# A planned two-layer decoder trunk on one core: score matmuls, weight splits and convolution chains are issued in another order

## The chip, the cores and the metric

The kernel runs on one core of one Trainium2 chip. The metric is the device time of one execution in microseconds (us); the kernel before takes 1359.83 us, the median of three runs (1359.78 to 1360.3).

## The reference, cut to what matters

Two layers work on 256 tokens of width 1024, all in float32. Each layer is, in this order, a SwiGLU feed-forward block (FFN1, inner width 2752), a mixer, a second SwiGLU block (FFN2) and a gated per-layer embedding (PLE); each block starts with an RMS norm and adds to the residual stream:

```python
z = u @ w_in                      # mLSTM q|k, v, o-gate, gates; SWA q, k, v; merge gates
m_qk = silu(causal_dwconv(m_qk, m_conv_w, m_conv_b))          # 4 taps
hm = mlstm_chunkwise(mq, mk, mv, ig, lf)                      # 4 heads of 256
ha = swa_gqa_sinks(aq, ak, av, a_sinks)                       # 16 query heads, 4 kv heads of 64
merged = sigmoid(g_m) * (hm @ w_branch_m) + sigmoid(g_a) * (ha @ w_branch_a)
h = h + merged @ w_out
```

## The kernel before, in words

Every float32 matrix product is made of three products of rounded halves: a value x is split into hi (a rounded copy) and lo = x - hi, and a product is hi·hi + hi·lo + lo·hi. The split of a weight part (128 rows by 1024 columns) takes one copy `wh` on ScalarE and one subtraction `wl` on VectorE; both read the tile `raw` that a DMA on the SyncE queue has filled. There are two raw tiles (`RAW`) and eight pairs of split tiles (`RING`). The same split is made of every activation that is multiplied, as `uT` (the normed, transposed residual), `qT` (queries of the window attention), `qk` (convolved queries and keys of the mLSTM) and `hmT` (output of the mLSTM heads).

The order of instructions on TensorE, ScalarE, VectorE and SyncE is that of the Python program, which carries a planner. `Clock` holds an estimated time for each engine; `now` is that of TensorE. Small work stands in generators ("chains") in the list `bg`: a chain issues one step, yields, and is due again when its step should be done. Between matmuls the program calls `tick()`, which advances every chain that is due and then calls `feed()`, which may begin the split of one more weight part: it issues `wh` and leaves a chain that will issue `wl`. `feed()` holds back while ScalarE's or VectorE's estimated end is more than 3.0 us past `now` (2.0 us once four parts are in store: `AHEAD`, `STORE`). `finish(chain)` is called where TensorE is about to need a chain's result; it moves the planner's clock to the next due time until the chain is done. When a raw tile's last `wl` has been issued, `prefetch()` issues the next load.

The chains that the change touches:

- `conv` (line 1158), 8 in each layer: four ScalarE activations in a first step for the two chains of a projection (`cv`, bias and last tap), then two steps of three VectorE multiply-adds each, a Silu on ScalarE (`cy`), and the split of the result (`qk`). `qk_job` starts two of them at the end of each of the four `z` projections. The key half ends in the chain `head`, which does an mLSTM head: `st` matmuls, weighting, `num` matmuls, a norm, transposes into `hmT`. Heads pass in order (`begun`, `turn`). The output gate `og` has to be there before `num`.
- `scores` (line 1361): for a block of 128 queries and a pair of kv heads. Two steps of 12 matmuls (two query heads, both kv heads) for the second block, one of 24 for the first. The queries' hi and lo halves are in `qT`; the two kv heads of a pair lie on different halves of the partitions.
- `norm` (line 639): after the last block of a layer and before the next FFN1 (`between`), it scales, then transposes (`to_T`) and splits into `uT`.

After the mixer's first two `z` projections comes `ya` (attention output times w_branch_a), then `og`, two more `z`, the gate `gt`, and `ym` (hm times w_branch_m, whose last k tiles are head 3's `hmT`).

Of the kernel before, what the change touches and what calls it, by code (L numbers as in the profile page):

```python
# [19 lines left out]
P = 128  # L20
# [14 lines left out]
RING = 8  # L35
STORE, HASTE = 4, 3
AHEAD = (3.0, 2.0)
ACTIVE = 5
LAG = 1.5
WARM = 5  # L40
# [126 lines left out]
class Trunk:  # L167
# [7 lines left out]
    def __init__(self, ctx, tc, a, out):  # L175
        self.tc, self.a, self.out = tc, a, out
        self.clock = Clock()
        self.nc = Core(self.clock, tc.nc)
        pool = lambda name, bufs, **k: ctx.enter_context(tc.tile_pool(name=name, bufs=bufs, **k))
        self.const = pool("const", 1)  # L180
        self.rawp = pool("raw", RAW)
        self.wp = pool("w", RING)
        self.slots = pool("slots", 22)
        self.gp = pool("g", 1)
        self.sc = pool("sc", 7)
        self.small = pool("small", 6)
        self.psum = pool("psum", 8, space=PSUM)
        self.dram = pool("dram", 1, space=bass.MemoryType.DRAM)
        self.n = 0
        self.jobs, self.bg, self.haste, self.second = [], [], False, None  # L190
        self.embedded, self.crossed, self.extra = {}, False, 0
        self.pending, self.loaded, self.store = deque(), deque(), 0
        self.free, self.raws = deque([0.0] * RING), deque([0.0] * RAW)
        self.consts()
# [5 lines left out]

    def tick(self):

        for chain in list(self.bg):
            if chain[1] <= self.clock.now:
                self.advance(chain)
        self.feed()

    def advance(self, chain):
        if chain not in self.bg:
# [3 lines left out]
            self.bg.remove(chain)  # L213
        chain[1] = self.clock.end(outer)

    def later(self, chain, ready=0.0):

        self.bg.append([chain, max(self.clock.done(), ready)])
        return self.bg[-1]

    def start(self, chain):
        chain = self.later(chain)
        self.advance(chain)
        return chain

    def finish(self, chain):
        while chain in self.bg:
            self.tick()
            ahead = [c[1] for c in self.bg if c[1] > self.clock.now]
            if ahead and chain in self.bg:  # L230
                self.clock.wait(min(ahead))

# [103 lines left out]
    def feed(self, must=False):  # L336

        clock = self.clock
        if not self.loaded or not self.free:
            return  # L340
        raw, parts = self.loaded[0]
        part, arrival = parts[0]
        slack = AHEAD[self.store >= STORE]
        if not must and max(self.free[0], arrival, clock.t["scalar"] - slack, clock.t["vector"] - slack) > clock.now:
            return
        if not must and (self.second is not None or self.haste and self.store >= HASTE + self.extra):
            return
        self.store += 1
        ready = max(self.free.popleft(), arrival)
        parts.popleft()  # L350
        last = not parts
        if last:
            self.loaded.popleft()
        w = part.k * part.n
        hi = self.wp.tile([P, QU], F32R, tag="wh", name=self.name("wh"))[:, :w]
        lo = self.wp.tile([P, QU], F32R, tag="wl", name=self.name("wl"))[:, :w]

        def chain():
            src = raw[:, part.c0 : part.c0 + w]
            if part.gain is not None:  # L360
                for j in range(part.k):
                    o = slice(j * part.n, (j + 1) * part.n)
                    self.nc.scalar.mul(hi[:, o], src[:, o], part.gain[:, j : j + 1])
                yield
                for j in range(part.k):
                    o = slice(j * part.n, (j + 1) * part.n)
                    self.nc.vector.scalar_tensor_tensor(lo[:, o], src[:, o], part.gain[:, j : j + 1],
                                                        hi[:, o].bitcast(F32), op0=ALU.mult, op1=ALU.subtract)
            elif part.rows is None:
                yield from self.splitting(hi, lo, src)  # L370
            else:
                self.tc.nc.gpsimd.memset(lo[part.rows.stop :].bitcast(F32), 0.0)
                self.nc.scalar.copy(hi, src)
                yield
                r = part.rows
                self.nc.vector.tensor_tensor(lo[r], src[r], hi[r].bitcast(F32), op=ALU.subtract)
            part.ready = clock.done()
            if last:
                self.raws.append(part.ready)
                self.prefetch()  # L380

        part.hi, part.lo = (x.rearrange("p (k n) -> p k n", k=part.k) for x in (hi, lo))
        part.chain = self.later(chain())
        outer = clock.begin(dma=ready)
        self.advance(part.chain)
        clock.end(outer)
        return part.chain

    def need(self, part):

# [248 lines left out]
    def norm(self, t, ss, g, xT, between):  # L639

        r = self.scale(ss)
        if between and t:
            self.clock.stage["late"] = self.clock.done() + LAG
        yield
        xn = [self.scaled(t, n, r, g) for n in range(2)]
        if between and t:
            self.clock.stage["late"] = self.clock.done() + LAG
        yield
        while between and not self.crossed:
            yield  # L650
        for n in range(2):
            self.to_T(xn[n], xT, n * 4, t)
        if t == 0:
            self.haste = False
# [395 lines left out]
class Mlstm:  # L1050
# [97 lines left out]
    def qk_job(self, w_in, part, hp):  # L1148

        c0 = part * D + hp * NB  # L1150
        unit = self.tr.unit(w_in, c0)

        def run():
            for i, ps in enumerate(self.tr.project_T(unit, self.xT, "z")):
                self.tr.start(self.conv(ps, part, 2 * hp + i, c0 // P + 2 * i))
        self.tr.jobs.append(run)

    def conv(self, ps, part, hd, f):
# [106 lines left out]
class Swa:  # L1265
# [83 lines left out]
    def groups(self, chains):  # L1349
        tr, acc = self.tr, {}  # L1350
        for p in range(2):
            for t in range(NT):
                while any(self.inputs.get(i, tr) is tr or self.inputs[i] in tr.bg
                          for i in [(0, s) for s in range(t + 1)] + [(p + 1, t)]):
                    yield
                while sum(c in tr.bg for c in chains) >= ACTIVE:
                    yield
# [3 lines left out]
    def scores(self, t, p, acc, chains):  # L1361


        tr, nc = self.tr, self.nc
        S = (t + 1) * P
        per = NB // S
        tok = slice(t * P, (t + 1) * P)
        rows = [slice(g * AD, (g + 1) * AD) for g in range(2)]
# [4 lines left out]
        for j0 in range(0, 4, per):  # L1373
            js = slice(j0, j0 + per)
            ps = [tr.bank("sc").rearrange("p (j s) -> p j s", j=per) for _ in range(2)]
            for j in range(per):
                for x, y in ((0, 0), (0, 1), (1, 0)):
                    for g in range(2):
                        nc.tensor.matmul(ps[g][:, j, :], self.qT[x](4 * p + j0 + j, tok, p=rows[g]),
                                         self.kT[rows[g], y, p, :S], start=j + x + y == 0, stop=x == 1,  # L1380
                                         skip_group_check=True)
            yield
            if t:
                for g in range(2):
                    nc.scalar.copy(pr[g][:, js, :], ps[g][:, :, P:])
                yield
            for g in range(2):
                if t:
                    above = tr.above.bitcast(mybir.dt.uint32)[:, None, :].to_broadcast([P, per, P])
                    nc.vector.copy_predicated(pr[g][:, js, :], above, ps[g][:, :, :P])  # L1390
                    nc.vector.tensor_reduce(mx[g][:, js], pr[g][:, js, :], axis=AX.X, op=ALU.max)
                else:
                    for j in range(per):
                        i = j0 + j
                        nc.vector.tensor_tensor_reduce(pr[g][:, i, :], ps[g][:, j, :], tr.band, 1.0, NEG, op0=ALU.add,
                                                       op1=ALU.max, accum_out=mx[g][:, i : i + 1])
                nc.vector.scalar_tensor_tensor(mx[g][:, js], mx[g][:, js], -0.125, self.nsink[:, hd[g]][:, js],
                                               op0=ALU.mult, op1=ALU.min)
            yield
            for g in range(2):  # L1400
                for j in range(per):
                    i = j0 + j
                    nc.scalar.activation(pr[g][:, i, :], pr[g][:, i, :], AF.Exp, scale=0.125, bias=mx[g][:, i : i + 1],
                                         accum_out=den[g][:, i : i + 1])
# [79 lines left out]
```

## Time and profile before

| what | value |
|---|---|
| median of three runs | 1359.83 us |
| the profiled execution's own time | 1359.88 us |
| its span, first to last instruction | 1358.2 us |
| TensorE matmul busy | 1350.5 us, 99% |
| VectorE busy | 903.0 us, 66% |
| ScalarE busy | 751.0 us, 55% |
| granted TensorE clock | 1.000 |
| chain that ended last | TensorE 97%, VectorE 2% |

The profiled execution lies 0.05 us above the median, and 1.7 us of its time lie outside the span. Matmul ends are modelled, and matmuls overlap; so the time that a wait costs is best read from starts: how much longer a group of matmuls takes from its start to the start of the next than the same group elsewhere. In the rows, "PE" is TensorE's matmuls, "PEld" its weight loads, "DVE" VectorE, "ACT" ScalarE; nearly all instructions carry line 133, the planner's helper, so the tile names tell them apart.

### The profile page before, as it was taken

Reading aid. Unit: us, or ns where it says so; the run is one execution under the profiler, and the core shown is the slowest. Engines: PE = TensorE matmul, PEld = TensorE weight load, DVE = VectorE, ACT = ScalarE, POOL = GpSimd, SP = SyncE. Lnnn points to the kernel's source line nnn. Section 1 sums busy time; section 2 is a strip of 40 time slices with the busy share of each in tenths; the row PEclk is TensorE's granted clock in tenths of the full one; section 3 lists DMA queues with packets and bytes.
Section 4 is the critical chain, followed back from the end, with each engine's and each line's share of the span. In section 5 each row is a group of like instructions: output and inputs, shape, how many; then the busy total and the mean of one; then the engine's idle time right before and its main releaser. Section 6 shows DMA issues by size and latency. Waiting matters only on the chain.

```text
span 1358.2 us, 22024 instructions
## 1 busy us (share of the span) xinstructions
PE 1350.5 (99%) x8974; PEld 1223.5 (90%) x8974; DVE 903.0 (66%) x1411; ACT 751.0 (55%) x1241; POOL 53.4 (4%) x82
## 2 busy tenths in 40 slices
PE   9999999999999999999999999999999999999998
PEld 7999887899899899988889998878998998999887
DVE  6766567888887755454665554578888877554545
ACT  6655446887565444443555443468875654444433
POOL 1000003000000000000000000030000000000000
PEclk9999999999999999999999999999999999999999
DMA  7755745354654475565466556463546554755651
GB/s 239 226 187 158 248 146 195 117 156 124 219 202 163 153 234 185 172 223 182 169 217 216 173 193 200 136 203 107 160 120 221 199 174 143 244 188 171 235 192 54
DMA packets 126789, 245.91 MB, mean 181 GB/s; under 512 B 15160, under 2 KB 24288, under 8 KB 126688
## 3 DMA queue, kind: packets, MB, share of 16 engines
q1 hardware_dynamic: 126672, 244.50, 55.9%
q8 instruction: 70, 1.15, 0.3%
q14 instruction: 31, 0.25, 0.1%
q10 hardware_dynamic: 16, 0.00, 0.0%
HBM read 242.39 MB, written 2.10 MB: 180 GB/s over the span
## 4 chain that ended last, share of the span: by engine, by line
PE 97%; DVE 2%; ACT 0%; DMA 0%; issue 0%; SPq 0%; DVEq 0%; ACTq 0%
PE dn L133 18%; PE pg L133 18%; PE pu L133 14%; PE gu L133 7%; PE gt L133 7%; PE z L133 7%; PE kvq L133 5%; PE og L133 3%; PE yo L133 3%; PE ym L133 3%; PE v L133 3%; PE tp L133 3%; PE ya L133 2%; PE sc L133 1%; DVE cv L133 1%; PE ha L133 1%
## 5 line engine op out<-in xcount | busy, mean ns | idle before, releaser
L133 DVE TENSOR_TENSOR wl<-raw,wh 128x1024 fp32r<-128x1024 f32 (+1 forms) x405 | 487.9, 1221 | 272.3 <-ACT wh L133 270.0
L133 ACT CAST wh<-raw 128x1024 fp32r<-128x1024 f32 x405 | 415.2, 1049 | 329.5 <-DMA raw<-in_ffn_w_down_dram 71.2
L133 PE MATMUL dn<-wh,hid 128*128 128x512 f32 x688 | 218.1, 395 | 0.0
L133 PE MATMUL pg<-uT,wh 128*128 128x256 f32 x1088 | 195.0, 282 | 0.0
L133 PE MATMUL pu<-uT,wh 128*128 128x256 f32 x1088 | 193.9, 281 | 0.0
L133 PEld LDWEIGHTS pg<-uT,wh 128*128 128x128 f32 x1088 | 166.8, 188 | 0.4
L133 PEld LDWEIGHTS pu<-uT,wh 128*128 128x128 f32 x1088 | 166.4, 188 | 0.0
L133 PEld LDWEIGHTS dn<-wh,hid 128*128 128x128 f32 x688 | 129.2, 188 | 30.7
L133 PE MATMUL pg<-uT,wl 128*128 128x256 f32 x544 | 152.6, 280 | 0.0
L133 PE MATMUL pu<-uT,wl 128*128 128x256 f32 x544 | 152.5, 280 | 0.0
L133 PE MATMUL dn<-wl,hid 128*128 128x512 f32 x352 | 139.2, 395 | 0.0
L133 PEld LDWEIGHTS pu<-uT,wl 128*128 128x128 f32 x544 | 102.7, 189 | 0.0
L133 PEld LDWEIGHTS pg<-uT,wl 128*128 128x128 f32 x544 | 102.7, 189 | 0.0
L133 PE MATMUL gt<-uT,wh 128*128 128x256 f32 x512 | 92.8, 282 | 0.0
L133 PE MATMUL z<-uT,wh 128*128 128x256 f32 x512 | 92.6, 283 | 0.0
L133 PE MATMUL gu<-wh,uT 128*128 128x512 f32 x256 | 81.4, 399 | 0.0
L133 PEld LDWEIGHTS gt<-uT,wh 128*128 128x128 f32 x512 | 79.1, 188 | 1.5
L133 PEld LDWEIGHTS dn<-wl,hid 128*128 128x128 f32 x352 | 66.1, 188 | 15.2
L133 PEld LDWEIGHTS z<-uT,wh 128*128 128x128 f32 x512 | 78.8, 188 | 0.6
L133 ACT ACTIVATE wh<-raw,gcol 128x512 fp32r<-128x512 f32 (+1 forms) x104 | 59.0, 638 | 29.0 <-DMA raw<-in_ffn_w_gate_dram 16.2
L133 DVE SCALAR_TENSOR_TENSOR wl<-raw,gcol,wh 128x512 fp32r<-128x512 f32 (+1 forms) x104 | 62.4, 654 | 17.6 <-ACT wh L133 17.6
L133 PE MATMUL z<-uT,wl 128*128 128x256 f32 x256 | 72.0, 281 | 0.0
(223 smaller groups left out, 2177.8 us busy)
## 6 DMA issues: line engine op xcount, KB each, us to landing
raw<-in_w_in_dram SPq DMA_DIRECT2D x60, 1024.0 KB
raw<-in_ffn_w_up_dram SPq DMA_DIRECT2D x40, 1024.0 KB
raw<-in_ffn_w_down_dram SPq DMA_DIRECT2D x40, 1024.0 KB
raw<-in_ffn_w_gate_dram SPq DMA_DIRECT2D x38, 1024.0 KB
raw<-in_w_branch_a_dram SPq DMA_DIRECT2D x16, 512.0 KB
raw<-in_w_branch_m_dram SPq DMA_DIRECT2D x8, 1024.0 KB
raw<-in_w_out_dram SPq DMA_DIRECT2D x8, 1024.0 KB
raw<-in_ple_gate_w_dram SPq DMA_DIRECT2D x8, 1024.0 KB
```

Of the source, the lines that this page charges most:

```text
L133: return issue(*args, **kw)
```

## The change

Three orders of issue change; no instruction is added or taken away by the program's text.

1. In `scores`, the matmuls with the queries' hi half are issued first for all query heads of a step, and those with the lo half after them. Before, each head's three products stood together.
2. Every chain that splits a weight part is kept in a list `feeds`. In a `between` norm, ahead of the transposes and the splits of their result, `settle()` advances each of them once: a split whose `wh` is issued then issues its `wl` at once.
3. The `conv` chains are marked `calm`. Their first step is issued as before; after that `tick()` passes over them while the later of ScalarE's and VectorE's estimated ends is more than `CALM` = 2.0 us past `now`. `finish()` also stops at the time at which this backlog comes down to 2.0 us.

```diff
--- before.py
+++ after.py
@@ -35,6 +35,7 @@
 RING = 8
 STORE, HASTE = 4, 3
 AHEAD = (3.0, 2.0)
+CALM = 2.0
 ACTIVE = 5
 LAG = 1.5
 WARM = 5
@@ -187,7 +188,7 @@
         self.psum = pool("psum", 8, space=PSUM)
         self.dram = pool("dram", 1, space=bass.MemoryType.DRAM)
         self.n = 0
-        self.jobs, self.bg, self.haste, self.second = [], [], False, None
+        self.jobs, self.bg, self.haste, self.second, self.feeds = [], [], False, None, []
         self.embedded, self.crossed, self.extra = {}, False, 0
         self.pending, self.loaded, self.store = deque(), deque(), 0
         self.free, self.raws = deque([0.0] * RING), deque([0.0] * RAW)
@@ -200,10 +201,14 @@
 
     def tick(self):
 
+
         for chain in list(self.bg):
-            if chain[1] <= self.clock.now:
+            if chain[1] <= self.clock.now and not (chain[2] and self.backlog() > CALM):
                 self.advance(chain)
         self.feed()
+
+    def backlog(self):
+        return max(self.clock.t["scalar"], self.clock.t["vector"]) - self.clock.now
 
     def advance(self, chain):
         if chain not in self.bg:
@@ -213,20 +218,21 @@
             self.bg.remove(chain)
         chain[1] = self.clock.end(outer)
 
-    def later(self, chain, ready=0.0):
-
-        self.bg.append([chain, max(self.clock.done(), ready)])
+    def later(self, chain, ready=0.0, calm=False):
+
+        self.bg.append([chain, max(self.clock.done(), ready), calm])
         return self.bg[-1]
 
-    def start(self, chain):
-        chain = self.later(chain)
+    def start(self, chain, calm=False):
+        chain = self.later(chain, calm=calm)
         self.advance(chain)
         return chain
 
     def finish(self, chain):
         while chain in self.bg:
             self.tick()
-            ahead = [c[1] for c in self.bg if c[1] > self.clock.now]
+            ahead = [c[1] for c in self.bg if c[1] > self.clock.now] + [self.clock.now + self.backlog() - CALM]
+            ahead = [x for x in ahead if x > self.clock.now]
             if ahead and chain in self.bg:
                 self.clock.wait(min(ahead))
 
@@ -381,10 +387,17 @@
 
         part.hi, part.lo = (x.rearrange("p (k n) -> p k n", k=part.k) for x in (hi, lo))
         part.chain = self.later(chain())
+        self.feeds.append(part.chain)
         outer = clock.begin(dma=ready)
         self.advance(part.chain)
         clock.end(outer)
         return part.chain
+
+    def settle(self):
+
+        for chain in self.feeds:
+            self.advance(chain)
+        self.feeds = []
 
     def need(self, part):
 
@@ -648,6 +661,8 @@
         yield
         while between and not self.crossed:
             yield
+        if between:
+            self.settle()
         for n in range(2):
             self.to_T(xn[n], xT, n * 4, t)
         if t == 0:
@@ -1152,7 +1167,7 @@
 
         def run():
             for i, ps in enumerate(self.tr.project_T(unit, self.xT, "z")):
-                self.tr.start(self.conv(ps, part, 2 * hp + i, c0 // P + 2 * i))
+                self.tr.start(self.conv(ps, part, 2 * hp + i, c0 // P + 2 * i), calm=True)
         self.tr.jobs.append(run)
 
     def conv(self, ps, part, hd, f):
@@ -1361,6 +1376,7 @@
     def scores(self, t, p, acc, chains):
 
 
+
         tr, nc = self.tr, self.nc
         S = (t + 1) * P
         per = NB // S
@@ -1373,12 +1389,11 @@
         for j0 in range(0, 4, per):
             js = slice(j0, j0 + per)
             ps = [tr.bank("sc").rearrange("p (j s) -> p j s", j=per) for _ in range(2)]
-            for j in range(per):
-                for x, y in ((0, 0), (0, 1), (1, 0)):
-                    for g in range(2):
-                        nc.tensor.matmul(ps[g][:, j, :], self.qT[x](4 * p + j0 + j, tok, p=rows[g]),
-                                         self.kT[rows[g], y, p, :S], start=j + x + y == 0, stop=x == 1,
-                                         skip_group_check=True)
+            for j, x, y in [(j, 0, y) for j in range(per) for y in range(2)] + [(j, 1, 0) for j in range(per)]:
+                for g in range(2):
+                    nc.tensor.matmul(ps[g][:, j, :], self.qT[x](4 * p + j0 + j, tok, p=rows[g]),
+                                     self.kT[rows[g], y, p, :S], start=j + x + y == 0, stop=x == 1,
+                                     skip_group_check=True)
             yield
             if t:
                 for g in range(2):
```

## Rows read from the trace of the kernel before

**Rows 1.** The page: span, and TensorE's busy time.
```profile
span 1358.2 us, 22024 instructions
PE 1350.5 (99%) x8974; PEld 1223.5 (90%) x8974; DVE 903.0 (66%) x1411; ACT 751.0 (55%) x1241; POOL 53.4 (4%) x82
```
**Rows 2.** Waits of TensorE's weight loads: waiting <- releaser: us in total, times, longest.
```profile
PEld ya L133 <- DVE wl L133: 1.2, 2, 0.6
...
PEld sc L133 <- DVE qT L133: 0.8, 2, 0.4
...
PEld ym L133 <- DVE hmT L133: 0.5, 2, 0.3
```
**Rows 3.** Timeline of PE, two score steps: start, length, what [idle before].
```profile
231.21 0.50 PE L133 MATMUL sc<-kT,qT 64*128 64x256 f32 x4
231.91 0.73 PE L133 MATMUL sc<-kT,qT 64*128 64x256 f32 x8 [0.20 <-DVE qT L133]
...
241.33 0.97 PE L133 MATMUL sc<-kT,qT 64*128 64x256 f32 x12
```
**Rows 4.** Timeline of DVE beside the first of these steps.
```profile
231.12 0.74 DVE L133 SCALAR_TENSOR_TENSOR qT<-tp,feat,qT 128x512 fp32r<-128x512 f32 x1
```
**Rows 5.** Timeline of PE at the start of layer 1's FFN1.
```profile
687.29 0.39 PE L133 MATMUL gu<-wl,uT 128*128 128x512 f32 x1
...
693.97 0.63 PE L133 MATMUL gu<-wh,uT 128*128 128x512 f32 x2
...
694.67 0.63 PE L133 MATMUL gu<-wh,uT 128*128 128x512 f32 x2
...
696.01 0.63 PE L133 MATMUL gu<-wh,uT 128*128 128x512 f32 x2
```
**Rows 6.** Timeline of DVE in the same stretch.
```profile
684.67 1.29 DVE L133 TENSOR_TENSOR uT<-tp,uT 128x512 fp32r<-128x512 f32 x2 [0.53 <-ACT uT L133]
...
689.60 1.23 DVE L133 TENSOR_TENSOR wl<-raw,wh 128x1024 fp32r<-128x1024 f32 x1
693.20 1.29 DVE L133 TENSOR_TENSOR uT<-tp,uT 128x512 fp32r<-128x512 f32 x2 [2.37 <-ACT uT L133]
694.40 1.21 DVE L133 TENSOR_TENSOR wl<-raw,wh 128x1024 fp32r<-128x1024 f32 x1
```
**Rows 7.** Timeline of ACT in the same stretch.
```profile
688.47 2.05 ACT L133 CAST wh<-raw 128x1024 fp32r<-128x1024 f32 x2
```
**Rows 8.** Timeline of PE in the projection ya of layer 0.
```profile
328.51 0.40 PE L133 MATMUL ya<-qT,wh 128*128 128x256 f32 x2
...
328.86 0.40 PE L133 MATMUL ya<-qT,wh 128*128 128x256 f32 x2
...
329.90 0.40 PE L133 MATMUL ya<-qT,wh 128*128 128x256 f32 x2
```
**Rows 9.** Timeline of DVE ahead of that wait.
```profile
325.03 2.93 DVE L133 SCALAR_TENSOR_TENSOR cv<-z,feat,cv 128x255 f32<-128x255 f32 x6
...
328.41 3.49 DVE L133 TENSOR_TENSOR wl<-raw,wh 128x1024 fp32r<-128x1024 f32 x3
```
**Rows 10.** Timeline of ACT ahead of that wait: two neighbouring groups of weight copies.
```profile
315.82 1.05 ACT L133 CAST wh<-raw 128x1024 fp32r<-128x1024 f32 x1
...
324.89 2.94 ACT L133 CAST wh<-raw 128x1024 fp32r<-128x1024 f32 x3
```
**Rows 11.** Windows: stretch, us, then busy of PE, PEld, DVE, ACT, POOL; clock; DMA.
```profile
317.00:330.00 13.00, 12.58 (x105) 12.38 (x104) 11.02 (x22) 12.93 (x21) 0.00 (x0) 1.00 0.38 83
```
**Rows 12.** Groups of ACT instructions, whole span: the table loads.
```profile
L133 ACT ACT_TABLE_LOAD x15 | 19.2, 1283 | 5.3 <-DVE cv L133 3.6 <-PEq L1473 1.4
```
**Rows 13.** The chain that ended last: head 2's score matmuls in layer 0.
```profile
405.14 1.18 PE st L133 x10
```
**Rows 14.** Timeline of DVE: head 2's keys split, and the last hmT of layer 0.
```profile
401.79 0.69 DVE L133 TENSOR_TENSOR qk<-cy,qk 128x512 fp32r<-128x512 f32 x1
...
433.70 0.42 DVE L133 TENSOR_TENSOR hmT<-tp,hmT 128x256 fp32r<-128x256 f32 x1 [0.37 <-ACT hmT L133]
```

## The prediction

> **What bounds the kernel now.** I read the page first. TensorE is busy for 1350.5 of 1358.2 us [rows 1] at full granted clock, and the chain that ended last is TensorE nearly throughout. A third engine's work can therefore be worth only what TensorE waits for it. So the second view is the list of waits, and in it the weight loads, since those meet a missing operand first [rows 2]. The waits in mid-kernel are few and short: twice 0.6 us of `ya` for a weight's lo half, twice 0.4 us of the scores for the queries' lo half, twice 0.25 us of `ym` for the last `hmT`. One of `gu` is read from the timeline below. Each pair is one wait per layer; the two layers issue the same program there. Third, the timelines round these places show what a wait costs in starts (a stopped stream also refills, so it costs more than the wait), and what stands ahead of the late instruction in its queue.
>
> **The change part by part.** All sums are against the profiled execution's own 1359.88 us, which is 0.05 us over the median; what lies outside the span I leave as it is. No instruction is added by the program text, so every term is a wait that goes or comes.
>
> **Scores, lo half last.** In the second block's first step, four score matmuls start at 231.21, and the fifth, the first with the queries' lo half, at 231.91 [rows 3]. VectorE issues that lo half at 231.12 and needs 0.74 us, to 231.86 [rows 4]. The group from 231.21 to the end of its last matmul takes 0.70 + 0.73 = 1.43 us, and an undisturbed one of 12 takes 0.97 us [rows 3]; the wait costs 0.46 us. With the change, eight hi matmuls stand ahead of the first lo one, not four. Twelve take 0.97 us; the step from four to eight is two more pairs, of about 0.12 us each (an estimate: 0.97 less 0.50 for the first four, over four pairs). So lo is first wanted 0.24 us later, at 231.21 + 0.22 + 0.24 + 0.22 = about 231.8, still some 0.1 us before it is there. Bounds: 0.24 us is gained if the refill stays, 0.46 if the short rest costs nothing. I take 0.24, the row being nearer to a wait that stays; for two layers **0.48 us**. The result of the step is no later than before, as the same 12 matmuls end it, and what reads it waits for the group.
>
> **Weight splits ahead of the norm's transposes.** This can act once, between the layers, since only the PLE of layer 0 is followed by a `between` norm. TensorE takes 693.97 to 694.67 = 0.70 us for three 512-wide matmuls, and 694.67 to 696.01 = 1.34 us for the next three [rows 5]: 0.64 us lost. The late operand is a `wl` at 694.40 to 695.61, issued behind the two `uT` subtractions at 693.20 [rows 6]. Its `wh` is the second of the pair on ScalarE that ends at 688.47 + 2.05 = 690.52 [rows 7]; the `wl` of the first runs at 689.60 to 690.83, and then VectorE stands idle for 2.37 us until ScalarE has done `uT` [rows 6]. Put ahead of the transposes, the second `wl` runs from 690.83 to about 692.0, wholly inside that idle time. So it costs nothing there, and gives all of **0.64 us**. If that cover were gone, `uT` would be late by one `wl`, 1.2 us, and the gain would become a loss of about that. The same call stands ahead of token block 0's transposes. There `uT` waits only 0.53 us on ScalarE at 684.67 [rows 6], so a `wl` of 1.2 us in front pushes it by up to 0.7, to end at about 686.6; the first matmul on its lo half comes after 687.29 [rows 5], so 0.7 us of cover is left. A raw tile is read out earlier, so its next load goes out earlier on the SyncE queue; nothing waits behind that which did not wait before. POOL's queue is not passed. What is late next is nothing that I see.
>
> **Conv chains stand back.** In `ya`, three matmuls take 328.51 to 328.86 = 0.35 us, and the next three 328.86 to 329.90 = 1.04 us [rows 8]: 0.69 us lost, in both layers 1.38 us. The late `wl` is issued at 328.41 and ends about 329.6; ahead of it stand six conv multiply-adds, 325.03 to 327.96, while its `wh` was the first of three that began on ScalarE at 324.89, done by 325.9 [rows 9, 10]. So VectorE could have made the `wl` 2.5 us earlier. Why it stood at the limit is seen one step back: between 315.82 and 324.89 no weight copy was begun at all [rows 10], while ScalarE was busy for 12.93 of 13 us and VectorE for 11.02 [rows 11]. The store of split parts ran empty while conv, Silu and their splits were issued freely. With fewer than four parts in store a split may begin at 3.0 us of backlog and a calm chain only at 2.0, so splits go first just when the store is low. The bounds: nothing (the six multiply-adds wait but other work fills the queue) to 1.38 us. A delay of one group of three multiply-adds, 1.47 us, is more than the wait, so I take all of it, **1.38 us**.
>
> What is queued behind: a held chain blocks nobody in a hardware queue, as it is not issued yet; but its own successors wait. For heads 0 and 1 there is room, since their `num` waits for the output gate, which is projected only after `ya`. For heads 2 and 3 there may be none: head 2's keys are split on VectorE at 401.79 to 402.48 [rows 14], its `st` starts at 405.14 [rows 13], and its chain runs through head 3 to the `hmT` at 433.70 [rows 14] for which `ym` already waits [rows 2]. There a held step can add to the wait. From below: a gain, if the split work is spread better, of at most the whole `ym` wait, some 0.36 us per layer with its refill (an estimate: 0.25 us and a refill of 0.11, as 0.58 became 0.69 in `ya`). From above: the three `wl` that stand together, 3.49 us [rows 9], all pass a critical conv step, in each layer. In between, the planner holds a chain only while 2.0 us of work are queued before it, so the engine is not idle for it, and once four parts are in store the splits have the same limit as the calm chains and gain no precedence. I take zero.
>
> ScalarE's table loads cost 1283 ns each, 15 in the kernel [rows 12]. The Trainium skill, ScalarE: Activation LUTs, in its section on table sets as the hidden batching unit, asks to batch calls by set, because each change of set loads tables; holding back Silus while Exps go on works against that. That section gives about 2.7 us for a load, by which two more would fill ScalarE for 5.4 us, an estimate; this trace shows 1.28 us a load, 2.57 us for two, and the trace decides. The sum is the same by both as long as the copies behind a load are not late; when they are, it is the rival below.
>
> **The sum.** 0.48 + 0.64 + 1.38 = 2.50 us; 1359.88 - 2.50 = **1357.4 us**. About 0.2%, here 2.7 us, is what a measurement of this kernel can tell from no change; the sum lies just inside.
>
> **The rivals.**
> *Late heads* (the other side). Held conv steps delay heads 2 and 3 by d in each layer, and `ym` waits d longer: 1357.4 + 2d. For it: the chain from 405.14 to 433.70 already ends in a wait. Against it: held work runs when the queue drains, so d is only what jumps ahead. With d = 1.25 the gain is gone; from d = 2.6 the kernel is slower by over 0.2%, at d = 3.49 it is 1364.4.
> *More table loads.* A Silu held past an Exp costs two more loads, 2.57 us of ScalarE, in a stretch where it is full [rows 11]; the weight copies behind them come late, and `ya` keeps its wait: 1357.4 + 1.38 = 1358.8.
> *The hold does not act.* With four or more in store both limits are 2.0 us, and the planner may see no backlog over 2.0 where the chip has one; the `ya` wait stays, also 1358.8.
> *More goes.* `ym`'s wait goes too (0.72) or the scores' wait goes wholly (0.44): 1356.2 to 1357.0.
>
> **How the numbers follow.** Forecast 0.50, late heads 0.17, table loads 0.10, no hold 0.10, more 0.13. Faster by over 0.2% (below about 1357.1): "more", and 0.15 out of the forecast's own spread of about 0.6 us: 0.28. Slower (above 1362.5): the upper half of late heads, 0.09. Within: 0.63. The range must leave out 0.2: below, 1356.3 cuts off the far end of "more"; above, 1360.6 takes in late heads up to d = 1.6. The forecast's own range is 1356.8 to 1358.0.
>
> **What would show it.** Right: at the two `ya` places the triple of 1.04 us becomes 0.35, and a weight copy is begun between the two groups of [rows 10]; `wl` ahead of `uT` near 691, and no `gu` wait; eight score matmuls ahead of a remaining short wait. Wrong: a `ym` wait above 1 us, more than 15 table loads, a new wait in the stream of `ya` or `og`, or a TensorE wait for a bank that a held conv still reads.

## The result and the profile after

The changed kernel takes 1364.16 us (median of seven runs, 1363.14 to 1366.16); seven runs of the kernel before give 1359.83 us. The ratio is 1.0034, with an interval of 1.0022 to 1.0045. The kernel became slower, by 4.3 us, and the time lies above the predicted range.

The page of the profiled execution, which took 1364.02 us, beside [rows 1]:

```profile
span 1361.9 us, 22040 instructions
...
PE 1351.0 (99%) x8974; PEld 1224.4 (90%) x8974; DVE 902.3 (66%) x1411; ACT 753.4 (55%) x1243; POOL 53.9 (4%) x82
```

TensorE's busy time is what it was, within 0.5 us; the span has grown by 3.7 us. So most of it, 3.2 us, is time in which TensorE waits, and the list of its waits says for what (waiting <- releaser: us in total, times, longest):

```profile
PE ym L134 <- ACT hmT L134: 2.6, 2, 1.5
PE ym L134 <- DVE hmT L134: 1.9, 2, 0.9
...
PE num L134 <- DVE mp L134: 0.5, 1, 0.5
```

**What went, as forecast.** The three waits that the change was costed on are gone or cut. The timeline of TensorE at the places of [rows 3] and [rows 8] (start, length, what):

```profile
231.43 1.20 PE L134 MATMUL sc<-kT,qT 64*128 64x256 f32 x12
...
328.49 0.40 PE L134 MATMUL ya<-qT,wh 128*128 128x256 f32 x2
...
328.84 0.40 PE L134 MATMUL ya<-qT,wh 128*128 128x256 f32 x2
...
329.20 0.40 PE L134 MATMUL ya<-qT,wh 128*128 128x256 f32 x2
```

The `ya` triples of 0.35 us follow each other without a gap, so about 0.69 us a layer is gained; and ScalarE begins weight copies at 317.70 and 324.10, in the stretch of [rows 10] that had none. The twelve score matmuls stand in one row of 1.20 us, where the wait for `qT` had split it; in starts the wait is +0.13 and +0.11 us in the two layers, where it was +0.36 and +0.35. On VectorE, ahead of layer 1's FFN1, both `wl` now stand before the `uT` subtractions, unlike [rows 6]; the `wh` of the second is on ScalarE, the transposes on TensorE:

```profile
691.85 1.22 DVE L134 TENSOR_TENSOR wl<-raw,wh 128x1024 fp32r<-128x1024 f32 x1
694.42 1.22 DVE L134 TENSOR_TENSOR wl<-raw,wh 128x1024 fp32r<-128x1024 f32 x1 [1.34 <-ACT wh L134]
695.56 1.28 DVE L134 TENSOR_TENSOR uT<-tp,uT 128x512 fp32r<-128x512 f32 x2
```
```profile
693.30 1.09 ACT L134 CAST wh<-raw 128x1024 fp32r<-128x1024 f32 x1
```
```profile
692.99 1.03 PE L134 MATMUL tp<-ident,xn 128*128 128x128 f32 x8
```

TensorE's `gu` stream has no wait there.

**What came.** At the end of each mixer `ym` waits for head 3's `hmT`, twice in each layer. TensorE in layer 0:

```profile
432.81 0.38 PE L134 MATMUL tp<-ident,og 128*128 128x128 f32 x2
434.31 0.38 PE L134 MATMUL ym<-hmT,wh 128*128 128x256 f32 x1 [1.11 <-ACT hmT L134]
435.63 0.39 PE L134 MATMUL ym<-hmT,wh 128*128 128x256 f32 x1 [0.94 <-DVE hmT L134]
```

ScalarE and VectorE in the same stretch show what is ahead of the two operands:

```profile
432.94 1.04 ACT L134 CAST wh<-raw 128x1024 fp32r<-128x1024 f32 x1 [0.26 <-PE ym L134]
433.89 0.37 ACT L134 CAST hmT<-tp 128x256 fp32r<-128x256 f32 x1
```
```profile
434.02 1.23 DVE L134 TENSOR_TENSOR wl<-raw,wh 128x1024 fp32r<-128x1024 f32 x1 [0.88 <-ACT wh L134]
435.16 0.42 DVE L134 TENSOR_TENSOR hmT<-tp,hmT 128x256 fp32r<-128x256 f32 x1
```

The transposes end at 433.19, and the 0.37-us copy that `ym` wants could begin then. It begins at 433.89, behind a weight copy `wh`; and the subtraction that makes the lo half stands behind that weight's `wl`. A begun weight split thus stands between the steps of the last transposition, on both engines. Before, the `hmT` subtraction ran at 433.70 with nothing but its own copy ahead of it [rows 14]. A split stood in that tail too, but in the first of its two transpositions, and no wait came of it. ScalarE, then TensorE, before:

```profile
430.68 1.05 ACT L133 CAST wh<-raw 128x1024 fp32r<-128x1024 f32 x1 [1.78 <-PE ym L133]
431.64 0.36 ACT L133 CAST hmT<-tp 128x256 fp32r<-128x256 f32 x1
433.30 0.37 ACT L133 CAST hmT<-tp 128x256 fp32r<-128x256 f32 x1 [1.29 <-PE tp L133]
```
```profile
432.88 0.38 PE L133 MATMUL tp<-ident,og 128*128 128x128 f32 x2
...
433.81 0.76 PE L133 MATMUL ym<-hmT,wh 128*128 128x256 f32 x2
```

Seven `ym` matmuls ran between the last transposes and the short wait, which lies inside the second of these rows; after the change none is left to run there. Layer 1 is the same after the change, and there the weight copy first waits for its load:

```profile
1114.05 1.04 ACT L134 CAST wh<-raw 128x1024 fp32r<-128x1024 f32 x1 [0.65 <-DMA raw<-in_w_out_dram]
1115.00 0.37 ACT L134 CAST hmT<-tp 128x256 fp32r<-128x256 f32 x1
```

In starts, `ym` loses 1.28 + 1.20 + 0.10 = 2.58 us in layer 0 and 1.65 + 1.20 + 0.11 = 2.96 us in layer 1, where it lost 0.36 in each. After the longer pair of waits the granted clock falls. Windows of layer 1 (stretch, us, busy of PE, PEld, DVE, ACT, POOL; clock; DMA):

```profile
1115.00:1117.00 2.00, 0.64 (x3) 0.45 (x4) 1.56 (x2) 0.37 (x2) 0.00 (x0) 1.00 0.83 307
1117.00:1119.00 2.00, 2.00 (x12) 2.00 (x12) 0.00 (x0) 0.00 (x0) 0.00 (x0) 0.53 0.54 205
1119.00:1121.00 2.00, 2.00 (x13) 2.00 (x13) 0.53 (x1) 0.00 (x0) 0.00 (x0) 0.61 0.00 0
1121.00:1125.00 4.00, 4.00 (x37) 4.00 (x36) 3.88 (x6) 2.51 (x3) 0.00 (x0) 1.00 0.00 0
```

That is the 1.2 GHz level for most of 4 us: 71 `ym` matmuls from 1116.74 on take 10.20 us, and the same 71 in layer 0, where the clock stayed at 1.00, take 8.56. So 1.6 us more are lost. Together with two waits of `num` in layer 1 (0.65 + 0.18 us in starts), the losses against before are 2.22 + 2.60 + 1.64 + 0.83 = 7.3 us and the gains 1.38 + 0.64 + 0.48 = 2.5; the balance of 4.8 stands against 3.7 us of span and 4.3 of the medians. The rest of about 1 us is spread over many small differences of pitch, and I did not place it.

### The profile page after: what moved, and what is told of

The parts are those of the page before. It is cut to its first block, busy times and chain, and to the rows that moved or that the text cites. A ratio compares the mean times of both kernels' runs of the same rounds, so it can differ in the third digit from the quotient of the medians.

```text
span 1361.9 us, 22040 instructions
## 1 busy us (share of the span) xinstructions
PE 1351.0 (99%) x8974; PEld 1224.4 (90%) x8974; DVE 902.3 (66%) x1411; ACT 753.4 (55%) x1243; POOL 53.9 (4%) x82
## 4 chain that ended last, share of the span: by engine, by line
PE 94%; DVE 3%; DMA 2%; ACT 1%; issue 0%; SPq 0%; POOL 0%; ACTq 0%; DVEq 0%
PE dn L134 18%; PE pg L134 17%; PE pu L134 14%; PE gu L134 7%; PE gt L134 5%; PE z L134 5%; PE kvq L134 5%; PE v L134 3%; PE ya L134 3%; PE og L134 3%; PE yo L134 3%; PE ym L134 2%; PE tp L134 2%; DVE wl L134 1%; PE sc L134 1%; DMA raw<-in_w_branch_m_dram 1%
```

## The experiments

The first four kernels take the change apart. **Theory one** was the prediction's rival: held `conv` steps of heads 2 and 3 make these heads late. **Theory two**: the hold on heads 0 and 1 moves the weight splits, and their new order makes the tail late. "Before" in this group took 1360.07 us.

**No hold** (`e12_no_calm`): parts 1 and 2 of the change stay.

```diff
-            if chain[1] <= self.clock.now and not (chain[2] and self.backlog() > CALM):
+            if chain[1] <= self.clock.now:
...
-            ahead = [c[1] for c in self.bg if c[1] > self.clock.now] + [self.clock.now + self.backlog() - CALM]
-            ahead = [x for x in ahead if x > self.clock.now]
+            ahead = [c[1] for c in self.bg if c[1] > self.clock.now]
```

> The change without its third part: scores and weight splits in the new order, no conv chain held. Both theories (held steps of heads 2 and 3; a hold on heads 0 and 1 that moves later weight splits) put the loss into the hold, so both expect a gain of 0.48 + 0.64 = 1.1 us: about 1358.7, ya waits of 0.69 us per layer and ym waits of 0.36 as before. If this kernel is slower than 1360.5, both fall and the loss lies in the first two parts.

Measured: 1358.82 us, ratio 0.9991 (0.9982 to 1.0): 1.25 us less than before. In starts, `ya` loses 0.60 and 0.57 us and `ym` 0.26 and 0.25, as before; here and with the other kernels of this section the refill of 0.10 us behind a wait is left out. The score and split terms are 0.48 + 0.64 = 1.12 us by the prediction, and the hold is the whole of the loss.

**The hold alone** (`e3_calm_alone`): `settle()` is not called, and the score matmuls go in the old order.

```diff
-        if between:
-            self.settle()
...
-            for j, x, y in [(j, 0, y) for j in range(per) for y in range(2)] + [(j, 1, 0) for j in range(per)]:
...
+            for j in range(per):
+                for x, y in ((0, 0), (0, 1), (1, 0)):
```

> The hold alone, scores and weight splits in the old order. Both theories expect the after kernel's time plus the 1.1 us that the other parts give back: 1364.2 + 1.1 = about 1365.3, with ym waits of 2 to 3 us per layer and no ya wait.

Measured: 1365.07 us, 1.0036 (1.0023 to 1.0048). `ym` loses 1.28 + 1.20 and 1.51 + 1.20 us; the score and `gu` waits are back at +0.36 and +0.53. The change in its two parts, -1.25 and +5.00 us, adds up to 3.75 of the 4.3 us.

**The hold on one pair of heads only** (`e5_hold_first`, `e7_hold_second`).

```diff
-                self.tr.start(self.conv(...), calm=True)
+                self.tr.start(self.conv(...), calm=hp == 0)    # e5; e7: hp == 1
```

> All of the change, but only the conv chains of heads 0 and 1 are held, those of heads 2 and 3 run as before. Theory one (the held steps of heads 2 and 3 come late): the loss goes, 1357.4 us, ym waits of about 0.36 us. Theory two (the hold on heads 0 and 1 moves the weight splits that follow, and one of them lands ahead of head 2's work in ScalarE's queue): nothing changes against the after kernel, about 1364, ym waits of 2 to 3 us.

> All of the change, but only the conv chains of heads 2 and 3 are held. Theory one: the loss stays and the ya wait comes back, 1364.2 + 1.4 = 1365.6. Theory two: the hold on heads 2 and 3 costs little, about 1358.7 to 1360 with ya waits of 0.69 and ym waits under 1 us per layer.

Measured: held heads 0 and 1, 1362.8 us, 1.0024 (1.0015 to 1.0033), with `ym` at 1.28 + 1.20 and 1.52 + 1.21. That is nearly the wait of the full change, though no step of heads 2 and 3 is held. Theory one falls. Held heads 2 and 3, 1368.75 us, 1.0066 (1.0054 to 1.0079), with `ym` at 2.08 + 1.20 and 2.07 + 1.21 and the `ya` waits back; theory two had this kernel at no loss, so it falls as it was put. What the two have in common is seen on ScalarE, here in the second:

```profile
433.90 1.04 ACT L134 CAST wh<-raw 128x1024 fp32r<-128x1024 f32 x1 [1.07 <-DMA raw<-in_w_out_dram]
434.85 0.36 ACT L134 CAST hmT<-tp 128x256 fp32r<-128x256 f32 x1
```

Whichever pair is held, a weight split stands in the last transposition (with heads 0 and 1 held, a `wh` at 432.63 ahead of the copy at 433.58). Three places remained for the cause. **A**: head 2's score copy `sl` stands behind a weight copy that waits for its load. After the change, ScalarE:

```profile
407.28 1.05 ACT L134 CAST wh<-raw 128x1024 fp32r<-128x1024 f32 x1 [3.68 <-DMA raw<-in_w_branch_m_dram]
408.24 0.26 ACT L134 COPY sl<-st 128x128 f32<-128x128 f32 x1
```

(before, `sl` ran at 406.36). **B**: the split in the tail itself. **C**: heads 2 and 3 come about 2 us later, whatever the tail looks like. The next four kernels shared their runs of before, 1359.86 us.

**Score copy first** (`e9_score_copy_first`): the whole change, and no new split is begun from head 2's key split to its score copy.

```diff
+        if part and hd == 2:
+            tr.stopped = True            # feed() begins no split while stopped, but one that is needed at once
...
+        tr.stopped = False               # after sl is issued
```

> All of the change, and no new weight split is begun from the split of head 2's convolved keys until head 2's copy of its score sums (sl) is issued, so that this copy stands ahead of the weight copy that waits for its load. Theory A (head 2 is late because its copy stands behind that weight copy on ScalarE, 3.7 and 5.4 us idle there): head 2 comes about 1.9 us earlier, ym's first wait (1.28 and 1.65 us) goes, the second (1.2 us per layer) may stay, the slow clock after the waits goes: 1359.5 to 1361. Theory B (the splits between the steps of the last hmT alone make the wait): unchanged, 1363 to 1364.

Measured: 1367.72 us, 1.0061 (1.0049 to 1.0074). `sl` runs at 405.68, 2.6 us earlier than after the change, and yet `ym` waits 2.61 + 1.21 and 2.68 + 1.20. A falls; but the time lies above what either theory had expected, and the run tells of head 2 alone: its output came 2.1 us earlier (`og` at 419.98 for 422.05), head 3's only 0.45 (429.00 for 429.45). ScalarE in the tail:

```profile
433.58 1.04 ACT L134 CAST wh<-raw 128x1024 fp32r<-128x1024 f32 x1 [1.59 <-DMA raw<-in_w_out_dram]
434.53 0.36 ACT L134 CAST hmT<-tp 128x256 fp32r<-128x256 f32 x1
```

**Quiet tail** (`e11_quiet_tail`): the whole change, and no new split from head 3's output until its last transposes are split.

```diff
+        tr.stopped = hd == MH - 1
         for t in range(NT):
             yield from tr.transposing(self.og[t][:, hd * MD : (hd + 1) * MD], self.hmT, 2 * hd, t, 2)
+        if hd == MH - 1:
+            tr.stopped = False
```

> All of the change, and no new weight split is begun from head 3's output to its last transposes, so that neither a weight copy nor its subtraction stands between the two steps of the last hmT. Theory B: ym's waits fall by what stood in between, about 0.7 us on ScalarE and 0.9 on VectorE per layer, and the slow clock goes: 1364.2 - 3.2 - 1.6 = about 1359.4. Theory A: the head stays late by some 2 us, and 1 to 2 us of wait per layer are left: 1361 to 1362. If nothing changes, 1364, both fall.

Measured: 1359.71 us, 0.9999 (0.999 to 1.0008), 4.45 us less than the changed kernel. TensorE and ScalarE in the tail of layer 0:

```profile
432.56 0.38 PE L134 MATMUL tp<-ident,og 128*128 128x128 f32 x2
433.40 0.85 PE L134 MATMUL ym<-hmT,wh 128*128 128x256 f32 x2 [0.46 <-ACT hmT L134]
```
```profile
432.97 0.37 ACT L134 CAST hmT<-tp 128x256 fp32r<-128x256 f32 x1 [0.55 <-PE tp L134]
433.24 2.00 ACT L134 CAST wh<-raw 128x1024 fp32r<-128x1024 f32 x2
```

The copy begins when its transposes are done, and the weight copies run behind it. `ym` loses 0.62 + 0.34 us in each layer, where the changed kernel lost 1.28 + 1.20 and 1.65 + 1.20; the clock stays at 1.000 throughout. The weights that were held back are late in the next block: `gu` waits 0.40 us in starts at 465.29 and again at 1144.19. B holds.

**Both** (`e15_both`): the two edits together.

> Both of these edits on all of the change. If A and B together make the loss, ym's waits come down to the 0.25 us of before or less, and the three parts' gains show: 1357 to 1358. If a third cause is at work, over 1360.

Measured: 1360.04 us, 1.0003 (0.9994 to 1.0012). `ym` loses 0.63 + 0.34 as with the quiet tail alone, so the earlier score copy brings nothing even then. The wait did not come down to the 0.25 us of before, and the time is at the edge that was set for a third cause.

**Second pair held, quiet tail** (`e13_second_quiet_tail`): `calm=hp == 1` and the quiet tail.

> The kernel that holds only the chains of heads 2 and 3 (1368.75 us), with the quiet tail of the run before. Theory B: its ym waits of 2.1 and 1.2 us per layer fall by about 1.6 together and the slow clock goes: 1363 to 1364. Theory A, which says that it is the late head: they fall by less than 1 us, 1366 or more.

Measured: 1362.17 us, 1.0017 (1.0007 to 1.0026), 6.6 us less than with the second pair held alone, more than expected; `ym` is at 0.63 + 0.34 here too. The last three kernels shared 1360.0 us for before.

**Splits wait for the convolutions** (`f4_splits_wait`): the whole change, and while the `conv` chains of heads 2 and 3 run, a split is begun only with fewer than three parts in store. It brings the heads back on time and leaves the tail as it comes.

```diff
+        if not must and self.store >= 3 and any(c in self.bg for c in self.convs):
+            return                       # in feed(); convs: the chains of heads 2 and 3
```

> All of the change; while a conv chain of heads 2 and 3 runs, a new weight split is begun only with fewer than three parts in store. Theory C (the hold on heads 0 and 1 pushes two to three weight splits out of the stretch 368 to 380 into 380 to 405, ahead of the conv steps of heads 2 and 3, so head 3's matmuls are issued some 2 us later against ym): heads come on time, ym's waits fall to 0.25 us or none and the three gains show, 1356.7 to 1358. Rival: the store runs low after the convs and gt or ym waits for a weight's lo half instead, over 1359.

Measured: 1360.55 us, 1.0007 (0.9998 to 1.0015). Head 2's `st` runs at 402.8 and the last transposes at 430.71, both some 2 us earlier than before the change, and `ym` still waits. TensorE, then ScalarE:

```profile
430.71 0.38 PE L134 MATMUL tp<-ident,og 128*128 128x128 f32 x2
...
433.36 0.38 PE L134 MATMUL ym<-hmT,wh 128*128 128x256 f32 x1 [0.16 <-ACT hmT L134]
434.68 0.39 PE L134 MATMUL ym<-hmT,wh 128*128 128x256 f32 x1 [0.94 <-DVE hmT L134]
```
```profile
431.99 1.05 ACT L134 CAST wh<-raw 128x1024 fp32r<-128x1024 f32 x1 [2.12 <-DMA raw<-in_w_out_dram]
432.94 0.36 ACT L134 CAST hmT<-tp 128x256 fp32r<-128x256 f32 x1
```

The transposes were done 1.8 us before the copy that reads them: it stood behind a weight copy that waited 2.12 us for its load. In starts, `ym` loses 0.32 + 1.21 and 0.42 + 1.21 us, and no `gt` or `ym` waits for a weight's lo half. So C alone is not the cause, but it has a share: heads in time take 0.95 and 1.22 us off `ym`'s wait, the clock stays at 1.00, and the time is 3.6 us below that of the change. By these figures a split in the last transposition costs 1.3 to 1.4 us a layer with the heads in time (1.53 and 1.63 for 0.26 and 0.25) and 1.5 to 1.9 with the heads late (2.48 and 2.85 for 0.96); late heads cost 0.7 without the split and 1.0 to 1.2 with it. The split is the larger part, and the two come together.

**Paired tail** (`f1_paired_tail`): the quiet tail, and head 3's transposes of both token blocks go together, both copies and then both subtractions.

```diff
+            ps = [tr.transposes(x, 2) for x in src]
+            yield
+            for hi, x in zip(his, ps):
+                nc.scalar.copy(hi, x)
+            yield
+            for lo, hi, x in zip(los, his, ps):
+                nc.vector.tensor_tensor(lo, x, hi.bitcast(F32), op=ALU.subtract)
```

> All of the change, the quiet tail, and head 3's transposes of both token blocks issued together, then both hi and both lo halves. The last hmT no longer hangs on a second round through three engines: ym's 1.07 us per layer of the quiet-tail run go, its gu waits of 0.4 us per layer stay: 1359.7 - 2.1 = 1357.6. If the late output of head 3 itself makes the rest, over 1359.

Measured: 1358.98 us, 0.999 (0.9982 to 0.9999), the fastest of the versions that keep the hold. `ym` loses 0.37 us in each layer, 0.11 and 0.12 more than before; `gu`'s two waits of 0.40 and one of `num` of 0.40 remain: 2.50 - 0.23 - 0.80 - 0.40 = 1.1 us below before by the terms, 1.02 measured. That lies between the two times that were expected.

**Paired tail without the hold** (`f3_no_calm_paired`): parts 1 and 2, the pairing, no quiet tail.

> No hold at all, scores and weight splits in the new order, and head 3's transposes of both blocks issued together: the ym waits of 0.36 us per layer go: 1358.8 - 0.7 = 1358.1; the ya waits of 0.69 us stay.

Measured: 1361.2 us, 1.0007 (0.9998 to 1.0016). `ym` has no wait of its own left, but TensorE's list of waits shows where it went:

```profile
PE yo L134 <- DVE mT L134: 1.0, 2, 0.5
PE ya L134 <- DVE wl L134: 0.8, 2, 0.4
PE gu L134 <- ACT uT L134: 0.5, 2, 0.2
```

`yo`, the next projection, now waits for the merged result (0.70 and 0.63 us in starts), and `gu` waits as well. Another order in the tail moved the splits again.

## Why the prediction was wrong

**Scores: right.** I took 0.24 us a layer; 0.23 and 0.24 were measured in starts, and the refill stays.

**Splits ahead of the norm's transposes: right in the number**, 0.64 us, **and lucky in the mechanism.** I had the second `wl` run inside VectorE's idle time, from 690.83. It ran at 694.42, after 1.34 us of waiting for its `wh`, which ScalarE began only at 693.30. So the `uT` subtractions began 2.57 us after their transposes (692.99 to 695.56), where it had been 1.26 us (691.94 to 693.20 [rows 6]): late by 1.3 us, the case that I had priced as a loss of about 1.2. No wait of `gu` followed, so TensorE had that much room, which I had not counted on. The kernel without the hold measures both terms together as 1.25 us, for 1.12.

**The hold, in `ya`: right.** The `ya` wait went in both layers, 1.38 us, and in the hold on the second pair alone it came back.

**The hold, in `ym`: this step failed.** "I take zero" was the term, and behind it "once four parts are in store the splits have the same limit as the calm chains and gain no precedence". The term measured -2.22 and -2.60 us in the two layers, and 1.64 us at the lower clock and 0.83 us of `num` came on top. Both bounds held for the wait itself (a loss of up to 3.49 us a layer), but I put the value at the wrong end. The mistake is one of place: I looked for work that is held, and asked whether the held work is late. What hurt most is work that is not held. With the hold on heads 0 and 1 alone a weight split comes to stand in head 3's last transposition, and costs `ym` most of a `wh` and a `wl`. Keeping splits out of that tail, with no other edit, takes the time from 1364.16 to 1359.71.

**Late heads** had the sign, the place and about the size: with the mean of the two terms, d = 2.4, its formula gives 1362.2, and with `num` and the clock 1364.7. Half of its mechanism was wrong: with no step of heads 2 and 3 held, the wait is nearly the same, and `ym` does not wait d longer for heads that are late by d. The heads are late, head 3's `og` by 2.1 us in layer 0 (427.37 to 429.45), and with the tail quiet that is worth 0.62 + 0.34 us of `ym` a layer, 0.7 us more than before. That its formula met the size is luck.

**More table loads** came, without the harm I gave them. The group of ScalarE's loads, beside [rows 12]:

```profile
L134 ACT ACT_TABLE_LOAD x17 | 21.8, 1283 | 1.7 <-PEq L1488 1.4
```

That is one more in each layer, and ScalarE is still busy for 12.90 of 13 us from 317 to 330; but `ya` has no wait. The Trainium skill, ScalarE: Activation LUTs, in its section on table sets as the hidden batching unit, asks to group calls by set; the number of loads rose as that rule has it. Each takes 1.28 us here, with the next activation right behind it (315.64, after a load from 314.35), and not the about 2.7 us of that section. No run here shows that they cost the kernel time.

**What stays open** is the path from the hold on heads 0 and 1 to the split's place. By the counts of `wl` on VectorE the splits shift: from 368 to 380 us six are made before and four after, from 380 to 405, while the convolutions of heads 2 and 3 run, eight and ten. The counts of their copies `wh` on ScalarE hardly do: five and five, eight and nine. That fits with a store that is filled later and at their expense, but no run isolates it. Why two versions came out worse than the change itself can be read from their tails: ScalarE stood idle longer ahead of the weight copy in front of the last `hmT`. It was 0.26 and 0.65 us in the two layers after the change, 1.07 and 1.07 with the second pair held, 1.59 and 1.66 with the earlier score copy, and `ym`'s first wait is 1.0 us more in each of the six. In both, the granted clock was also 0.50 from 437 to 441 and from 1122 to 1124 us. Why that copy comes later in them stays open.

## What to carry to other kernels

In a program whose order comes from a planner, a local hold is not local: it can shift the phase of everything that is issued when there is room, and what matters is which of it lands in front of the last operand that the busiest engine wants, and how much other work that engine has left by then. So where a change holds or moves work, look in the trace for the places at which that engine already waits a little for an operand (here `ym`, 0.25 us), and ask what else may be issued between the steps of the chain that makes it. Protect such a chain before tuning upstream of it: with the tail quiet and paired the hold cost nothing any more, but the kernel was no faster than with the two small edits alone (1358.98 and 1358.82 us).

## What was not expected of the hardware

After two waits of TensorE close together the granted clock fell at some places and not at others, and the length of the waits does not say where. In the changed kernel, after 1.49 and 0.94 us of standing idle with one matmul between them, it was 0.53 and 0.61 in the next two windows of 2 us; after 1.11 and 0.94 us it stayed at 1.00. With the hold on heads 0 and 1 alone it was the other way round: after 1.11 and 0.94 us in layer 0 it fell, after 1.35 and 0.94 us in layer 1 it stayed. Windows of that kernel, layer 0 and then layer 1:

```profile
436.00:438.00 2.00, 2.00 (x14) 2.00 (x13) 0.00 (x0) 0.00 (x0) 0.00 (x0) 0.65 0.16 60
438.00:440.00 2.00, 2.00 (x11) 2.00 (x10) 1.65 (x3) 0.56 (x1) 0.00 (x0) 0.50 0.00 0
...
1118.00:1120.00 2.00, 2.00 (x19) 2.00 (x18) 0.28 (x1) 0.00 (x0) 0.00 (x0) 1.00 0.38 142
```

The fall costs the changed kernel 1.6 us, more than either wait of that pair. The times of the changed kernel spread over 3.0 us, with mean clocks of 0.997 to 0.999 over the span, and those of before over 0.9 us. So what such a pair costs seems to differ from run to run; only one run of each kernel has a trace.

A copy on ScalarE that waits for its load holds up what is behind it. ScalarE stood idle for 3.68 us ahead of the copy at 407.28 after the change, and `sl` behind it came 1.9 us later than before; it stood idle for 2.12 us ahead of the copy in front of `hmT` in the kernel whose heads were in time, 0.9 us of them after the transposes were done. By its own length such a copy would cost 1.05 us.
